# Two of four weight-block sums made in DRAM by a copy and an adding transfer, raw weights in tiles of 512 columns

## The chip, the cores and the metric

The kernel runs on one core of one Trainium2 chip. The metric is device time in microseconds (us) of one execution. Three runs of the kernel before gave 2002.77, 2003.87 and 2006.32 us; the median, 2003.87, is what the change is measured against.

## What is computed

One inference step of a two-layer encoder on 512 prompt and 32 sample positions (544 columns in the kernel), width 1024, all in fp32. Each layer is a half-step FFN, a mixer (pooling, short convolution, differential attention) with its projections, and a second half-step FFN, each followed by a LayerNorm of the scaled residual. The part that the change touches is the FFN's first product, `x @ w_in`:

```python
def swiglu(x, w_in, w_out):
    gate, up = jnp.split(x @ w_in, 2, axis=-1)
    return (jax.nn.silu(gate) * up) @ w_out

# encoder_layer, for each of DEPTH=2 layers (D_MODEL=1024, D_FF=2816)
x = layer_norm(ALPHA * x + 0.5 * swiglu(x, w_ffn_in[0], w_ffn_out[0]), ln_g[0], ln_b[0])
proj = x @ w_in
...
x = layer_norm(ALPHA * x + mix, ln_g[1], ln_b[1])
x = layer_norm(ALPHA * x + 0.5 * swiglu(x, w_ffn_in[1], w_ffn_out[1]), ln_g[2], ln_b[2])
```

## The kernel before

Features lie on the 128 partitions, positions on the free axis, cut in two halves of 272 columns. To keep fp32 accuracy every operand is split in a rounded high part and the remainder (`whi`, `wlo` for weights, `xh`, `xl` for activations), and each product takes three matmuls of 128 x 272: hi by hi, lo by hi, hi by lo. ScalarE rounds (L172 for weights), VectorE subtracts (L173).

Weights stream through one class, `Weights`, as a list of units in the order of use. A unit of kind "t" is a plain weight tile. A unit of kind "s" is one of the FFN's 22 column blocks from the fourth on (NPLAIN = 3): its weights are four blocks of 128 x 512 (b11, b12, b22, b21), and the function `seven` (L332, matmuls at L341) makes the 2 x 2 block product with seven products in place of eight, 84 matmuls. That needs four sums of weight blocks: r1 = b11 + b12, r2 = r1 + b22, r3 = b12 + b22 and r2 + b21, made by VectorE with `add` (L198, tiles `sum`), and sums of the activations (class `Blocks`, L316 to L319), made by VectorE when an FFN begins. There are 19 such units in each of four FFNs, 76 in all; they come in groups of six or seven, between which eight tiles of the FFN's second product (w2) stand.

Raw weights land in tiles `raw` of 128 x 1024, three of them (RAW_BUFS), by transfers that SP issues: L190 for plain tiles, L205 for the two of a sum unit. A raw tile is free again when its last `wlo` is made. The ten pairs of `whi` and `wlo` (W_BUFS) come free as TensorE uses them. So SP mostly waits for raw tiles.

Between FFNs stands a LayerNorm (class `LN`). Its last steps for the two halves go through all engines: VectorE centres and scales (z, L431), ScalarE applies gain and bias and rounds (L433, L438), POOL makes `xl` (L439), and TensorE begins the next weights' products on each of eight feature tiles as it comes (function `start`; three units at once). POOL has little else: rstd (L412), the LayerNorm's sums (L380, L381, L388) and small work in the mixer. A plain FFN block's activation is L591 (ScalarE) and L592 (VectorE), a sum unit's L552 to L567; the first of these, L552, copies a product to the tile `up`, and the third product, which adds to the same accumulator, waits for it. The split of an FFN's hidden tiles is L287 (hh) and L288 (hl).

The order of the instructions on each engine is set by the framework's scheduler from the written order and from priorities, and is fixed when the kernel is built. Each engine and each issuing queue works in order. At the start `first` (L215) loads three units and the activations in pieces; then SP loads parameters, and two small inputs of the bias table (L619, L620). The bias table itself is written to DRAM and spread there by one transfer (scr<-rows, L629).

Of the kernel before, what the change touches and what calls it, by code (L numbers as in the profile page):

```python
# [10 lines left out]
F32 = mybir.dt.float32  # L11
# [5 lines left out]
P = 128  # L17
# [18 lines left out]
FB = 5  # L36
W_BUFS = 10
RAW_BUFS = 3
# [10 lines left out]
G = 512  # L49
# [24 lines left out]
def encoder_kernel(  # L74
# [82 lines left out]
    class Weights:  # L157
# [4 lines left out]
        def __init__(self, units):  # L162
            self.units, self.used, self.loaded, self.ready = units, 0, 0, []

        def fetch(self):
            return wp.tile([P, 2 * G], F32, tag="raw", name="raw", bufs=RAW_BUFS)

# [14 lines left out]
        def load(self):  # L182
            kind, src, n = self.units[self.loaded]
            self.loaded += 1
            if kind == "t":
                raw = self.fetch()
                c = 0
                for part in src if isinstance(src, tuple) else (src,):
                    w = part.shape[-1]
                    nc.sync.dma_start(out=raw[:, c:c + w], in_=part)  # L190
                    c += w
                self.ready.append(Tile([self.group(raw[:, g:min(g + G, n)]) for g in range(0, n, G)]))
            else:
                self.ready.append(self.sums(src))

        def add(self, a, b):
            r = big["pool"].tile([P, G], F32, tag="sum", name="sum", bufs=4)
# [3 lines left out]
        def sums(self, src):  # L201

            raws = [self.fetch() for _ in range(2)]
            for i, raw in enumerate(raws):
                nc.sync.dma_start(out=raw, in_=src[:, 2 * i * G:2 * (i + 1) * G])  # L205
            b11, b12, b22, b21 = (raw[:, c:c + G] for raw in raws for c in (0, G))
            g11, g21 = self.group(b11), self.group(b21)
            r1 = self.add(b11, b12)
            r2 = self.add(r1, b22)
            g2, g1 = self.group(r2), self.group(r1)  # L210
            g3 = self.group(self.add(b12, b22))
            g22 = self.group(b22)
            return g11, g21, g2, g1, g3, g22, self.group(self.add(r2, b21))

        def first(self, x):  # L215

            units = self.units[:NSTART]
            raws = [self.fetch() for _ in units]
            tiles = [[self.new_group() for _ in range(2)] for _ in units]
            n = 2  # L220
            for i in range(NK // n):
                ks, cs = slice(n * i, n * i + n), slice(n * i * P, n * (i + 1) * P)
                nc.scalar.dma_start(out=ya[:, ks, HS[0]], in_=xT[:, ks, HS[0]])
                for raw, (_, src, _) in zip(raws, units):
                    o = slice(cs.start % G, cs.start % G + n * P)
                    nc.sync.dma_start(out=raw[:, cs], in_=src[cs.start // G][:, o])
            for i in range(NK // n):
# [926 lines left out]
```

## Time and profile before

| | |
|---|---|
| median of three runs | 2003.87 us (2002.77 to 2006.32) |
| profiled execution | 2006.03 us, its span 2004.2 us |
| TensorE, VectorE, ScalarE, POOL busy | 98%, 72%, 50%, 11% of the span |
| DMA | 189.12 MB moved, 94 GB/s in the mean |

The span runs from the first to the last instruction; 1.8 us of the execution's time lie outside it. Matmuls are pipelined, so one that lasts 0.29 us starts 0.125 us after the one before it, and the rate of starts tells more than busy time. A line of the profile is a line of the kernel before; PEld is TensorE's weight load, DVE is VectorE, ACT is ScalarE. In the order of the changed kernel, lines from 39 on have moved by some lines (L198 is now L223, L173 is L182, L439 is L459).

### The profile page before, as it was taken

The page shows a single profiled execution, that of the slowest core. Times are in us where ns is not written, and L with a number is a line of the kernel's source. Part 1 is how long each engine was busy: PE and PEld are TensorE (multiplying, and loading weights), DVE is VectorE, ACT ScalarE, POOL GpSimd, SP SyncE. Part 2 cuts the span into 40 slices and gives each one's busy share as a digit, 9 for nine tenths or more (in the row PEclk, how much of TensorE's full clock was granted, in tenths as well). Part 3 has the DMA queues.
Part 4 walks back from the last instruction along what each step waited for, and adds up shares of the span by engine and source line. Part 5 has one row for each costly group of instructions (what it writes and reads, how often), then busy time and mean ns, then how long its engine had stood idle before and what let it go on. Part 6 is the DMA issues. An engine that isn't in the chain of part 4 may idle for free.

```text
span 2004.2 us, 38173 instructions
## 1 busy us (share of the span) xinstructions
PE 1973.7 (98%) x15446; PEld 1937.3 (97%) x15446; DVE 1449.9 (72%) x2806; ACT 993.6 (50%) x2000; POOL 225.6 (11%) x214
## 2 busy tenths in 40 slices
PE   9999999999999999999999999999999999999997
PEld 9999999999899999999999999999899999999997
DVE  7958677677658967768798496775865698576676
ACT  6625445465436544535466254454754366355453
POOL 0000000510134000000420000015001330000003
PEclk9999999999899999999999999999999999999999
DMA  6332323142121242323223223232421213323231
GB/s 208 113 102 95 99 83 116 64 144 92 59 81 63 87 123 67 116 85 102 89 73 108 85 93 109 85 106 72 140 98 54 85 50 99 106 85 109 89 98 46
DMA packets 65834, 189.12 MB, mean 94 GB/s; under 512 B 9428, under 2 KB 15188, under 8 KB 65656
## 3 DMA queue, kind: packets, MB, share of 16 engines
q1 hardware_dynamic: 55584, 172.07, 27.4%
q10 hardware_dynamic: 10072, 14.60, 2.3%
q8 instruction: 121, 1.98, 0.4%
q14 instruction: 57, 0.47, 0.1%
HBM read 179.88 MB, written 8.34 MB: 94 GB/s over the span
## 4 chain that ended last, share of the span: by engine, by line
PE 90%; DVE 6%; issue 1%; ACT 1%; DMA 1%; POOL 1%; POOLq 0%; ACTq 0%; DVEq 0%
PE b L341 39%; PE b L255 30%; PE b L259 15%; DVE wlo L173 1%; PE b L778 1%; PE b L777 1%; DVE sum L198 1%; PE b L793 1%; PE b L419 1%; DVE z L431 1%; ACT ya L433 1%; PE b L865 1%; PE b L758 0%; DMA raw<-in_w 0%; PE b L405 0%
## 5 line engine op out<-in xcount | busy, mean ns | idle before, releaser
L172 ACT ACTIVATE whi<-raw 128x512 fp32r<-128x512 f32 (+2 forms) x586 | 357.3, 614 | 495.6 <-PE b L259 299.1
L173 DVE TENSOR_TENSOR wlo<-raw,whi 128x512 fp32r<-128x512 f32 (+2 forms) x586 | 408.8, 700 | 149.0 <-ACT whi L172 144.2
L255 PE MATMUL b<-hh,wlo 128*128 128x272 f32 x1408 | 405.7, 288 | 0.0
L255 PE MATMUL b<-hh,whi 128*128 128x272 f32 x1408 | 405.1, 288 | 0.0
L259 PE MATMUL b<-hl,whi 128*128 128x272 f32 x1408 | 404.7, 287 | 0.0
L255 PE MATMUL b<-xh,whi 128*128 128x272 f32 x1024 | 296.3, 297 | 10.0 <-ACT xh L438 9.1
L172 ACT ACTIVATE whi<-sum 128x512 fp32r<-128x512 f32 x304 | 190.7, 631 | 201.4 <-PE b L259 99.5
L255 PE MATMUL b<-xh,wlo 128*128 128x272 f32 x1024 | 290.1, 290 | 0.1
L173 DVE TENSOR_TENSOR wlo<-sum,whi 128x512 fp32r<-128x512 f32 x304 | 207.8, 689 | 87.4 <-ACT whi L172 80.4
L259 PE MATMUL b<-xl,whi 128*128 128x272 f32 x1024 | 265.7, 290 | 0.0
L255 PEld LDWEIGHTS b<-hh,whi 128*128 128x128 f32 x1408 | 265.0, 188 | 0.0
L255 PEld LDWEIGHTS b<-hh,wlo 128*128 128x128 f32 x1408 | 264.9, 188 | 0.0
L259 PEld LDWEIGHTS b<-hl,whi 128*128 128x128 f32 x1408 | 264.9, 188 | 0.0
L341 PE MATMUL b<-xh,wlo 128*128 128x272 f32 x912 | 262.6, 288 | 0.0
L341 PE MATMUL b<-xh,whi 128*128 128x272 f32 x912 | 262.2, 288 | 0.0
L341 PE MATMUL b<-xl,whi 128*128 128x272 f32 x912 | 261.8, 287 | 0.0
L255 PEld LDWEIGHTS b<-xh,whi 128*128 128x128 f32 x1024 | 195.1, 191 | 14.0 <-ACT xh L438 11.7
L255 PEld LDWEIGHTS b<-xh,wlo 128*128 128x128 f32 x1024 | 195.5, 191 | 0.6 <-DVE wlo L173 0.3
L259 PEld LDWEIGHTS b<-xl,whi 128*128 128x128 f32 x1024 | 182.3, 190 | 0.7 <-issue 0.5
L341 PE MATMUL b<-s56h,whi 128*128 128x272 f32 x608 | 175.4, 289 | 3.3 <-ACT up L552 3.3
L388 POOL TENSOR_TENSOR ya<-ya,shift 128x544 f32<-128x544 f32 x14 | 25.3, 1830 | 1355.4 <-DVE wlo L173 1313.9
L341 PE MATMUL b<-s73h,wlo 128*128 128x272 f32 x608 | 175.3, 288 | 0.0
(208 smaller groups left out, 4248.1 us busy)
## 6 DMA issues: line engine op xcount, KB each, us to landing
raw<-in_w SPq DMA_DIRECT2D x184, 512.0 KB, 3.8
raw<-in_w SPq DMA_DIRECT2D x64, 448.0 KB, 3.3
raw<-in_wi SPq DMA_DIRECT2D x40, 512.0 KB, 3.2
raw<-in_w SPq DMA_DIRECT2D x42, 256.0 KB, 3.3
raw<-in_wo SPq DMA_DIRECT2D x16, 512.0 KB, 3.2
U<-scr ACTq DMA_DIRECT2D x8, 320.0 KB, 3.5
out_nkT<-k ACTq DMA_DIRECT2D x8, 272.0 KB, 2.1
out_nvT<-vT ACTq DMA_DIRECT2D x8, 272.0 KB, 2.2
```

The source lines that it names most:

```text
L172: S.activation(out=hi, in_=raw, func=AF.Copy)
L173: V.tensor_tensor(out=lo, in0=raw, in1=hi.bitcast(F32), op=ALU.subtract)
L198: V.tensor_tensor(out=r, in0=a, in1=b, op=ALU.add)
L255: PE.matmul(acc[:, :HALF], v, x[k][0][:, HS[h]], start=first and i == 0, stop=False)
L259: PE.matmul(acc[:, :HALF], w.at(k)[0], x[k][1][:, HS[h]], start=False, stop=last)
L341: PE.matmul(acc[:, :HALF], v[:, cs], x, start=opens and j == 0 and m == 0, stop=j == len(xs) - 1 and m == 2, skip_group_check=True)
L388: POOL.tensor_tensor(out=c, in0=c, in1=self.s, op=ALU.subtract)
L419: PE.matmul(b[:, c * CH:(c + 1) * CH], self.rstd[h][:, c:c + 1].to_broadcast([CH, P]), ident[:CH, :CH], start=True, stop=True)
L431: V.tensor_tensor(out=z, in0=c, in1=self.rstd[h], op=ALU.mult)
L433: S.activation(out=c, in_=z, func=AF.Identity, bias=b, scale=g)
L777: PE.matmul(g[:, :w], qc[c][parts[c], qs], kh[parts[c], :w], start=True, stop=False)
L778: PE.matmul(g[:, :w], qc[c][:, qs], kc[c][:, :w], start=False, stop=True)
```

## The change

For the sum units from the third on (SUMS_FROM = 2), r1 and r3 are made in DRAM: SP copies b11 and b12 side by side into a DRAM tile `r13` of 128 x 1024 (L215), and POOL issues a transfer that adds b12 and b22 to it (L219). Both are written some units ahead (six and three), with a ring of eight DRAM tiles. The unit then loads five tiles of 128 x 512: b11, b21, b22 and the two halves of `r13`, and VectorE makes two sums, r2 and r2 + b21. All raw weights now land in tiles of 512 columns, seven of them, each by a transfer of its own. The mixer's buffers `f` go from five to four (FB), the `sum` buffers from four to three, and the bias table's two small loads go from SP's queue to ACT's.

```diff
@@ -33,9 +33,13 @@
 NB = 2
 NSTART = 3
 AHEAD = 300
-FB = 5
+SUMS_AHEAD = (6, 3)
+SUMS_FROM = 2
+FB = 4
 W_BUFS = 10
-RAW_BUFS = 3
+RAW_BUFS = 7
 FEED = (12, 5, 8)
 POOL_STATE = 15
 POOL_WINDOWS = (2, 4, 8, 16)
@@ -161,9 +165,14 @@
         def __init__(self, units):
             self.units, self.used, self.loaded, self.ready = units, 0, 0, []
-        def fetch(self):
-            return wp.tile([P, 2 * G], F32, tag="raw", name="raw", bufs=RAW_BUFS)
+            self.r13, self.ring = {}, []
+            self.todo = [[i for i, u in enumerate(units) if u[0] == "s"][SUMS_FROM:] for _ in range(2)]
+        def fetch(self, src):
+            raw = wp.tile([P, G], F32, tag="raw", name="raw", bufs=RAW_BUFS)[:, :src.shape[-1]]
+            nc.sync.dma_start(out=raw, in_=src)
+            return raw
         def new_group(self):
             return tuple(wp.tile([P, G], F32R, tag=n, name=n, bufs=W_BUFS) for n in ("whi", "wlo"))
@@ -182,56 +191,67 @@
         def load(self):
             kind, src, n = self.units[self.loaded]
             self.loaded += 1
+            self.sums_ahead()
             if kind == "t":
-                raw = self.fetch()
-                c = 0
-                for part in src if isinstance(src, tuple) else (src,):
-                    w = part.shape[-1]
-                    nc.sync.dma_start(out=raw[:, c:c + w], in_=part)
-                    c += w
-                self.ready.append(Tile([self.group(raw[:, g:min(g + G, n)]) for g in range(0, n, G)]))
+                parts = src if isinstance(src, tuple) else [src[:, g:min(g + G, n)] for g in range(0, n, G)]
+                self.ready.append(Tile([self.group(self.fetch(part)) for part in parts]))
             else:
-                self.ready.append(self.sums(src))
+                self.ready.append(self.seven(src, n, self.r13.pop(self.loaded - 1, None)))
+        def sums_ahead(self):
+            for ahead, todo, step in zip(SUMS_AHEAD, self.todo, (self.copy, self.accumulate)):
+                if todo and todo[0] < self.loaded + ahead:
+                    step(todo.pop(0))
+        def copy(self, i):
+            _, src, n = self.units[i]
+            if len(self.ring) < SUMS_AHEAD[0] + 2:
+                t = dram.tile([P, 2 * G], F32, name=f"r13_{len(self.ring)}")
+            else:
+                t = self.ring.pop(0)
+            self.ring.append(t)
+            self.r13[i] = t[:, :2 * n]
+            nc.sync.dma_start(out=self.r13[i], in_=src[:, :2 * n])
+        def accumulate(self, i):
+            _, src, n = self.units[i]
+            POOL.dma_start(out=self.r13[i], in_=src[:, n:3 * n], accum_op=ALU.add)
         def add(self, a, b):
-            r = big["pool"].tile([P, G], F32, tag="sum", name="sum", bufs=4)
+            r = big["pool"].tile([P, G], F32, tag="sum", name="sum", bufs=3)[:, :a.shape[-1]]
             V.tensor_tensor(out=r, in0=a, in1=b, op=ALU.add)
             return r
-        def sums(self, src):
-            raws = [self.fetch() for _ in range(2)]
-            for i, raw in enumerate(raws):
-                nc.sync.dma_start(out=raw, in_=src[:, 2 * i * G:2 * (i + 1) * G])
-            b11, b12, b22, b21 = (raw[:, c:c + G] for raw in raws for c in (0, G))
+        def seven(self, src, n, r13):
+            blocks = [src[:, :n], src[:, 3 * n:], src[:, 2 * n:3 * n]]
+            blocks += [src[:, n:2 * n]] if r13 is None else [r13[:, :n], r13[:, n:]]
+            b11, b21, b22, *b = (self.fetch(v) for v in blocks)
             g11, g21 = self.group(b11), self.group(b21)
-            r1 = self.add(b11, b12)
+            r1, r3 = b if b[1:] else (self.add(b11, b[0]), self.add(b[0], b22))
             r2 = self.add(r1, b22)
-            g2, g1 = self.group(r2), self.group(r1)
-            g3 = self.group(self.add(b12, b22))
-            g22 = self.group(b22)
+            g2, g1, g3, g22 = (self.group(v) for v in (r2, r1, r3, b22))
             return g11, g21, g2, g1, g3, g22, self.group(self.add(r2, b21))
...
@@ -616,8 +636,8 @@
     def build_bias(bp):
         rb = bp.tile([32, HEADS], F32, name="rb")
         oh = bp.tile([32, BL], F32, name="oh")
-        nc.sync.dma_start(out=rb, in_=relb)
-        nc.sync.dma_start(out=oh, in_=c_one)
+        nc.scalar.dma_start(out=rb, in_=relb)
+        nc.scalar.dma_start(out=oh, in_=c_one)
         vec = bp.tile([HEADS, BL], F32, name="vec")
         for q in range(2):
             acc, qs = bank(), slice(q * (BL // 2), (q + 1) * (BL // 2))
@@ -1023,7 +1043,7 @@
                     if i < NPLAIN:
                         units += [("t", (src[:, a * G:(a + 1) * G], src[:, b * G:(b + 1) * G]), 2 * G) for a, b in ((0, 3), (1, 2))]
                     else:
-                        units.append(("s", src, 4 * G))
+                        units.append(("s", src, G))
                 else:
                     c0, n = sum(FSPLIT[:i]) * P, FSPLIT[i] * P
                     units += [("t", w2[l, f, m, :, c0:c0 + n], n) for m in range(NK)]
```

The first place is VectorE where the second FFN of layer 0 begins: the last split of the weights before it (`wlo`), LayerNorm's `z`, the sums of the first sum unit, and the block sums of the activations (`s_...`). Before:

```order
L173 TENSOR_TENSOR wlo<-raw,whi 128x512
L411 TENSOR_SCALAR var<-var 68x4
L198 TENSOR_TENSOR sum<-raw 128x512
L431 TENSOR_TENSOR z<-ya,b 128x272 x8
L198 TENSOR_TENSOR sum<-sum,raw 128x512
L198 TENSOR_TENSOR sum<-raw 128x512
L198 TENSOR_TENSOR sum<-sum,raw 128x512
L316 TENSOR_TENSOR s_8052<-ya 128x272
L318 TENSOR_TENSOR s_8053<-ya 128x272
```

After:

```order
L182 TENSOR_TENSOR wlo<-raw,whi 128x512
L431 TENSOR_SCALAR var<-var 68x4
L451 TENSOR_TENSOR z<-ya,b 128x272 x8
L223 TENSOR_TENSOR sum<-raw 128x512
L223 TENSOR_TENSOR sum<-sum,raw 128x512
L336 TENSOR_TENSOR s_8261<-ya 128x272
L338 TENSOR_TENSOR s_8262<-ya 128x272
```

The adds r1 and r3 are gone: r2 (`sum<-raw`) and r2 + b21 stand behind the eight `z`, and the rest follows as before. The same pair is gone from the second unit, some 35 instructions later.

The second place is POOL in the LayerNorm ahead of that FFN. `xl` is the activations' remainder, eight tiles for each half. Before:

```order
L381 TENSOR_TENSOR acc_7261<-acc_7261,sq 128x544
L412 TENSOR_TENSOR rstd<-var,mhalf 68x4
L439 TENSOR_TENSOR xl<-ya,xh 128x272 x8
L412 TENSOR_TENSOR rstd<-var,mhalf 68x4
L439 TENSOR_TENSOR xl<-ya,xh 128x272 x8
L388 TENSOR_TENSOR ya<-ya,shift 128x544 x2
```

After, with `r_1_364` and the like as DRAM tiles of the ring:

```order
L432 TENSOR_TENSOR rstd<-var,mhalf 68x4
L459 TENSOR_TENSOR xl<-ya,xh 128x272 x8
L432 TENSOR_TENSOR rstd<-var,mhalf 68x4
L459 TENSOR_TENSOR xl<-ya,xh 128x272 x4
L219 DMA r_1_364<-in_w 128x1024
L459 TENSOR_TENSOR xl<-ya,xh 128x272 x4
L219 DMA r_2_437<-in_w 128x1024
L219 DMA r_3_567<-in_w 128x1024
```

One adding transfer now stands between the fourth and the fifth `xl` of the second half; the others of the FFN follow behind the eighth. The same stands ahead of the next two FFNs.

The third place is SP, from the mixer's weights (`in_wi`, `in_wo`) to the third sum unit of that FFN, after the change:

```order
L174 DMA raw<-in_wi 128x512 x40
L174 DMA raw<-in_wo 128x512 x16
L174 DMA raw<-in_w 128x512 x15
L174 DMA raw<-r_1_364 128x512 x2
L215 DMA r_1_364<-in_w 128x1024
L174 DMA raw<-in_w 128x512 x3
L174 DMA raw<-r_2_437 128x512 x2
L174 DMA raw<-in_w 128x512 x3
```

The copy into a ring tile stands right behind the loads from it for the unit that used it last, so the sums are begun eight units ahead.

## Rows read from the trace of the kernel before

**Rows 1.** The page: span, and busy time of each engine.

```profile
span 2004.2 us, 38173 instructions
...
PE 1973.7 (98%) x15446; PEld 1937.3 (97%) x15446; DVE 1449.9 (72%) x2806; ACT 993.6 (50%) x2000; POOL 225.6 (11%) x214
```

**Rows 2.** Windows: us; PE, PEld, DVE, ACT, POOL busy; granted clock; DMA share; GB/s.

```profile
160.00:230.00 70.00, 70.00 (x562) 70.00 (x561) 58.87 (x105) 42.62 (x80) 0.00 (x0) 1.00 0.34 102
634.00:665.00 31.00, 29.74 (x238) 29.52 (x237) 30.93 (x54) 21.89 (x44) 6.87 (x7) 1.00 0.21 66
```

**Rows 3.** Chain of waits, 655 to 666 us: start, us, what.

```profile
659.67 0.61 DVE sum L198
...
661.51 0.58 DVE sum L198
...
663.18 0.66 ACT hh L287
...
664.36 0.29 ACT up L552
...
664.70 1.39 PE b L341 x9
```

**Rows 4.** Timeline of TensorE (PE, then weight loads PEld), 663 to 666 us.

```profile
663.15 0.29 PE L341 MATMUL b<-xl,whi 128*128 128x272 f32 x1
...
664.70 0.19 PEld L341 LDWEIGHTS b<-s56h,whi 128*128 128x128 f32 x1 [1.48 <-ACT up L552]
```

**Rows 5.** Waits of TensorE's weight loads: us in total, times, longest.

```profile
PEld b L341 <- ACT up L552: 3.9, 3, 1.5
```

**Rows 6.** All instructions on tiles sum and raw: duration ns min/median/max.

```profile
L198 DVE TENSOR_TENSOR sum<-raw x152: 673/689/1267, 32.2 to 1918.3; 128x512 f32<-128x512 f32 x152
...
L205 SPq DMA_DIRECT2D raw<-in_w x152: 327/328/332, 21.4 to 1912.0; - x152
```

**Rows 7.** Timeline of VectorE, 626 to 642 us.

```profile
625.96 1.26 DVE L173 TENSOR_TENSOR wlo<-raw,whi 128x512 fp32r<-128x512 f32 x1
...
627.61 0.80 DVE L173 TENSOR_TENSOR wlo<-raw,whi 128x512 fp32r<-128x512 f32 x1
...
628.40 0.68 DVE L198 TENSOR_TENSOR sum<-raw 128x512 f32<-128x512 f32 x1
631.15 2.87 DVE L431 TENSOR_TENSOR z<-ya,b 128x272 f32<-128x272 f32 x8 [2.08 <-PE b L419]
...
635.13 1.26 DVE L198 TENSOR_TENSOR sum<-raw 128x512 f32<-128x512 f32 x1
```

**Rows 8.** DMA issues: KB each, median us to landing; window with the bias table's copy.

```profile
raw<-in_w SPq DMA_DIRECT2D x184, 512.0 KB, 3.8
...
raw<-in_w SPq DMA_DIRECT2D x42, 256.0 KB, 3.3
...
scr<-rows ACTq DMA_DIRECT2D x1, 1536.0 KB, 8.7
...
36.00:41.00 5.00, 5.00 (x43) 5.00 (x42) 5.00 (x11) 4.53 (x9) 0.00 (x0) 1.00 0.88 266
```

**Rows 9.** Timelines of POOL (xl) and TensorE, 632 to 643 us.

```profile
633.14 7.88 POOL L439 TENSOR_TENSOR xl<-ya,xh 128x272 fp32r<-128x272 f32 x8 [3.19 <-ACT xh L438]
...
635.80 2.40 POOL L439 TENSOR_TENSOR xl<-ya,xh 128x272 fp32r<-128x272 f32 x2
...
641.51 0.91 PE L259 MATMUL b<-xl,whi 128*128 128x272 f32 x6
```

**Rows 10.** Instructions on rstd (POOL) and on scr (issue by ACT), ns min/median/max.

```profile
L412 POOL TENSOR_TENSOR rstd<-var,mhalf x12: 1002/1014/1388, 375.8 to 1993.9; 68x4 f32<-68x4 f32 x12
...
L684 ACTq DMA_DIRECT2D U<-scr x8: 332/338/1434, 402.7 to 1457.9; - x8
```

**Rows 11.** Windows behind two equal waits of TensorE (columns as rows 2).

```profile
382.68:386.60 3.92, 3.92 (x22) 3.92 (x23) 3.37 (x7) 3.92 (x10) 3.42 (x4) 0.70 0.37 138
999.35:1003.00 3.65, 3.65 (x32) 3.62 (x33) 3.38 (x7) 3.65 (x10) 3.16 (x4) 1.00 0.46 150
```

More of the change, by code (lines that the diff above doesn't have):

```diff
@@ L217, in first @@
             units = self.units[:NSTART]
-            raws = [self.fetch() for _ in units]
+            raws = [[wp.tile([P, G], F32, tag="raw", name="raw", bufs=RAW_BUFS) for _ in range(2)] for _ in units]
             tiles = [[self.new_group() for _ in range(2)] for _ in units]
             n = 2
-            for i in range(NK // n):
-                ks, cs = slice(n * i, n * i + n), slice(n * i * P, n * (i + 1) * P)
+            cuts = [(n * i * P // G, slice(n * i * P % G, n * i * P % G + n * P)) for i in range(NK // n)]
+            for i, (g, cs) in enumerate(cuts):
+                ks = slice(n * i, n * i + n)
                 nc.scalar.dma_start(out=ya[:, ks, HS[0]], in_=xT[:, ks, HS[0]])
                 for raw, (_, src, _) in zip(raws, units):
-                    o = slice(cs.start % G, cs.start % G + n * P)
-                    nc.sync.dma_start(out=raw[:, cs], in_=src[cs.start // G][:, o])
-            for i in range(NK // n):
-                cs = slice(n * i * P, n * (i + 1) * P)
-                o = slice(cs.start % G, cs.start % G + n * P)
+                    nc.sync.dma_start(out=raw[g][:, cs], in_=src[g][:, cs])
+            for i, (g, cs) in enumerate(cuts):
                 for k in range(n * i, n * i + n):
@@ L232, in first @@
                 for raw, groups in zip(raws, tiles):
-                    hi, lo = groups[cs.start // G]
-                    self.part(raw[:, cs], hi[:, o], lo[:, o])
+                    hi, lo = groups[g]
+                    self.part(raw[g][:, cs], hi[:, cs], lo[:, cs])
             self.loaded, self.ready = len(units), [Tile(g) for g in tiles]
```

## Prediction

> **What bounds the kernel now.** I read the page's head first: TensorE is busy 98% of a span of 2004.2 us, VectorE 72% [rows 1]. A busy TensorE may still be waiting, so next come the windows, for the rate of its matmuls. In the 70 us from 160, a stretch of sum units (one column block of the first FFN product made with seven products), 562 matmuls run: one per 0.125 us, with no gap, while VectorE is busy 58.9 of 70 us and the DMA engines 0.34 of the time [rows 2]. There the kernel is bound by TensorE, and nothing that VectorE is spared can show. A unit is 7 x 4 x 3 = 84 matmuls, 10.5 us. The stretch 634 to 665 is different: 238 matmuls in 31 us, with VectorE busy 30.93 of 31.00 [rows 2]. This is the start of the second FFN of layer 0: LayerNorm is still being applied, the block sums of the activations (L316 to L319) are made, and the weights of the first sum units are prepared, all on VectorE. The chain of waits from 655 on shows what that does to TensorE: VectorE adds, an activation pair, ScalarE's split, its copy `up`, then matmuls [rows 3]. TensorE starts a matmul at 663.15 and the next at 664.70, released by `up` [rows 3, 4]. The waits list has three such waits, 3.9 us in all, the longest 1.5 [rows 5]; the two others end at the same place of the next two FFNs. Those 3.9 us are what a lighter VectorE can give back.
>
> **What the change takes away.** 74 of the 76 sum units lose two of their four adds, r1 and r3: 148 adds at 0.689 us [rows 6], 102 us of VectorE. In the stretches at TensorE's full rate that is worth nothing, since TensorE is the bound there. At the three places it counts. Of the first unit's four adds the one at 628.40 ran while VectorE waited for LayerNorm anyway (the next instruction, z, starts at 631.15), so its loss is free; the one at 635.13 took 1.26 us in the middle of the backlog [rows 7]. Of the second unit's four adds in the chain, two go, 0.61 and 0.58 us [rows 3]. In all about 2.4 us of backlog against a wait of 1.48 at most, so each wait should vanish; with the second unit's pair alone (1.2 us) the most that would be left is 0.3. The matmul starts give the loss: 664.70 - 663.15 less one spacing of 0.125 is 1.42, where the weight-load row reads 1.48 idle [rows 3, 4]; scaled to 3.9, **-3.7 us**. Bounds: -4.0 and, if only the second pair counts, -3.2.
>
> **What it adds, on SP.** Each sum unit now loads five tiles of 256 KB where it loaded two of 512 KB, and every other weight tile comes in two pieces: 832 SP transfers against 382, each 0.328 us of SP [rows 6], 148 us more on a queue that only waits for buffers otherwise. A copy stands behind the two loads of the ring buffer that it overwrites, so SP stands still until those land (3.3 us for 256 KB [rows 8]), with three raw loads of the unit after it queued behind. Seven raw buffers at five per 10.5 us hold 14.7 us of work; the cover is that slack. I take 0. If it is gone, a unit waits a few tenths, which is rival three's country.
>
> **What it adds, on POOL.** The accumulating transfers are issued from POOL, each after a wait for its copy. By the order all but three of them stand between LayerNorms, where POOL is idle. Three stand inside LayerNorm's second half, between the fourth and the fifth `xl`. Eight `xl` run from 633.14 for 7.88 us; the fourth and fifth end at 638.20, so POOL reaches the accumulate at about 637.0 and the eighth ends at 641.02 [rows 9]. TensorE reads the last two tiles from 641.51, the last one three matmuls (0.375 us) later, at 641.9 [rows 9]: 0.9 us to spare. Is the copy there by 637.0? Its ring buffer's second load needs the raw buffer freed by the wlo that ends at 628.41 [rows 7], lands 3.3 later at 631.7, and the copy then starts. Nothing in the trace is a copy of this size between DRAM tensors; the nearest is the bias table's, three times as large, 8.7 us [rows 8]. So 2.9 (a third) to 8.7; I take 3.8, the landing of a 512 KB load [rows 8], and have 635.5: before 637.0, so no wait. The issue itself is not in the trace either: between 0.33 us (a transfer issued by ACT) and 1.4 us (POOL's own smallest arithmetic, rstd, at its longest; median 1.0) [rows 10]. I take 1.0, the nearest on the same engine: 0.1 beyond the slack, three times, **+0.3 us**; bounds 0 and +1.5.
>
> **The rest.** The two bias loads move to ACT's queue, ahead of four splits: 2 x 0.34 us of ACT [rows 10], at a time when TensorE has three units' worth of weights in hand: 0, at most +0.7. FB 4, three sum buffers: the same order of instructions on POOL in the mixer, 0. DRAM traffic per unit grows from 1.05 MB to 1.31 of loads, 0.52 of copy and 0.52 (if an accumulate costs as a copy) to 1.57 (two reads and a write): 2.4 to 3.4 MB in 10.5 us. At 0.34 for 102 GB/s, and 0.88 for 266 while the bias table's copy runs [rows 2, 8], the engines move some 300 GB/s: 3.15 MB in 10.5 us. So the share goes to 0.75 to 1.08. The ring's eight buffers are filled far ahead, and between groups of six or seven sum units stand eight tiles of the second product; a load may land after 11 instead of 3.3 us before the 14.7 us of buffers run out (2 to 3 us of it is the split's). I take 0.
>
> **Sum.** 2006.03 - 3.7 + 0.3 = 2002.6, against the profiled execution's own time. That one lies 2.16 above the median of the three runs, 2003.87; on the median's scale the forecast is **2000.5 us**. Its own range, from the bounds above and one drop of the clock more or less, is 1998.5 to 2004. Such a drop: after a wait of the same 2.4 us the granted clock's mean was 0.70 in one place (part of it at the lower of the two levels, 1.2 GHz), with 22 matmuls in 3.92 us, and 1.00 in another, with 32 in 3.65 [rows 11]; it costs about 1.4 us where it falls.
>
> **Rivals.**
> *One: the waits stay.* VectorE's r2 now needs the ring buffer's tile, and everything at L316 to L319 stands behind it. Its load needs the raw tile freed by the wlo that ends at 627.2 and lands by 630.5; VectorE asks for it at 634.0, behind the eight z [rows 7]: 3.4 us to spare, which a load slowed by copies and accumulates could use up. Or an accumulate's issue is held while VectorE works, or holds it, as the adds and `xl` hold each other: an add takes 0.68 alone and 1.26 beside `xl` [rows 7]. One such hold per issue (1.26) costs 3 x 1.3 and eats the gain. Time: 2003.9, as before. For it: VectorE is never idle there. The Trainium skill, "SBUF — State Buffer", section "Who interferes with whom", warns that descriptors of a POOL transfer cannot be written while VectorE runs a two-port copy, and excepts tensor_tensor with two SBUF inputs, which it lets contend with POOL's reads alone. The trace agrees for reads (0.68 against 1.26); by that rule this half of the rival would fall and the forecast's 2000.5 stand. 0.22.
>
> *Two, slower: POOL stands in LayerNorm.* If the copy lands more than 5.2 us after its issue, POOL waits for it with four `xl` behind, and TensorE behind those, one for one. At the far bound of 8.7: 631.7 + 8.7 + 1.0 = 641.4 for the fifth `xl` instead of 637.0, 4.4 late, 3.5 beyond the slack, three times: +10.5, less 3.7: 2010.7. For it: TensorE has no other work in that place. Against it: DMA is 0.21 busy there [rows 2]. 0.18.
>
> *Three: the DMA engines.* At the upper bound of 1.08, 0.26 MB per unit are left over, 0.9 us; with nothing hidden, 74 x 0.9 = 64 us: about 2065. It decides where raw loads take over 11 us to land. The Trainium skill's page "DMA: Bandwidth & Descriptors", section "Issuing engines are not separate DMA queues", says that transfers of all issuers interleave on the same 16 engines, which speaks against this change: by it POOL's queue brings no bandwidth of its own, and the 64 us are the bound. The trace agrees as far as it goes, for SP's and ACT's transfers together (0.88 busy). Against it: the upper bound counts every passage of an accumulate at the price of a load, and the ring's lead of eight units has to be used up first. 0.07.
>
> *Four: not what it says.* The order shows 156 adds left of 304 and the copies eight units ahead, more than the six written. 0.01.
>
> **Chances.** Forecast 0.52, the rivals 0.22, 0.18, 0.07, 0.01. A measurement of this kernel tells 0.2%, 4 us, from no change: below 1999.86 is faster, above 2007.88 slower. A sum of 3.4 us lies next to the bound, so about half of the forecast is below 1999.86: faster 0.27. Same: the other half, the first rival, the fourth and the small cases of the second, 0.49. Slower: most of the second and the third, 0.24. The range leaves out the third rival and a tail at the low end: 1997 to 2011.
>
> **What would show it.** Right: 156 adds at the seven-product weights, no wait of L341's weight loads on `up` at the three places, 0.34 of DMA share grown to 0.75 or more with matmuls still at 0.125 us, `xl` at the three places with one gap of 1 us. Wrong: a POOL wait for a copy there, a wait of TensorE for whi or wlo inside sum units, raw loads that land after more than 11 us.

## Result and profile after: slower by 2.2%

The changed kernel took 2050.05 us in the median of four runs (2047.96 to 2050.34), the kernel before 2005.09 us on the same chip. The ratio is 1.0223, its 95% interval 1.0206 to 1.0241: slower by 45 us, where 2000.5 was forecast in a range from 1997 to 2011. The profiled execution took 2047.96 us.

The page of the changed kernel: span, busy time, DMA share in 40 slices, and two DMA queues (packets, MB, share of 16 engines); q1 is what SP issues, q0 the accumulates that POOL issues.

```profile
span 2046.2 us, 39606 instructions
...
PE 1986.7 (97%) x15446; PEld 1945.2 (95%) x15446; DVE 1365.4 (67%) x2658; ACT 995.4 (49%) x2000; POOL 281.6 (14%) x288
...
DMA  9966748333222665757428576662421228565331
...
q1 hardware_dynamic: 120576, 230.19, 37.3%
q0 software_dynamic: 10656, 38.80, 11.8%
```

Against [rows 1], VectorE is 84 us lighter, as the change meant, and the span is 42 us longer. So VectorE's time was not what was lost. Where it was lost the windows tell: the first 110 us of the kernel before, then the same 110 us and 70 us of sum units of the changed kernel (columns as in [rows 2]).

```profile
0.00:110.00 110.00, 107.66 (x827) 105.52 (x828) 92.17 (x190) 71.43 (x141) 0.20 (x4) 1.00 0.53 163
```

```profile
0.00:110.00 110.00, 95.44 (x674) 92.30 (x675) 74.92 (x158) 59.41 (x119) 10.15 (x16) 0.92 0.94 259
...
187.00:257.00 70.00, 65.86 (x507) 65.64 (x507) 48.21 (x88) 38.61 (x73) 4.06 (x5) 0.95 0.74 187
```

In the first 110 us 674 matmuls start instead of 827; 153 at 0.125 us are 19 us. In the 70 us from 187 it is 507 instead of the 562 that start in 70 us of sum units of the kernel before [rows 2], 6.9 us, and this was the kind of stretch in which TensorE had no gap before. The DMA engines are busy 0.94 and 0.74 of the time, where it was 0.53 and 0.34.

What TensorE waits for is in the waits of the changed kernel (L223 is the add, L587 a step of a sum unit's activation that reads its fifth product, L361 the matmuls of `seven`, L182 the split into `wlo`, L215 the copy, L174 the raw loads; SPq is SP's queue).

```profile
DVE sum L223 <- DMA raw<-r: 131.4, 57, 6.4
PEld b L361 <- DVE sg L587: 26.5, 21, 4.4
...
PEld b L361 <- DVE wlo L182: 5.6, 2, 5.2
...
SPq L215 <- DMA raw<-r: 102.7, 41, 5.4
```

VectorE waits 131 us for loads of the ring's tiles, and TensorE for `sg` of VectorE, a wait that [rows 5] did not have beside it; once, at 73.69 us, it waits 5.2 us for the `wlo` of a sum unit. How the one makes the other is in VectorE's timeline, 220 to 231 us, and in the chain of waits of the same place.

```profile
220.21 0.69 DVE L182 TENSOR_TENSOR wlo<-raw,whi 128x512 fp32r<-128x512 f32 x1
227.32 0.69 DVE L223 TENSOR_TENSOR sum<-raw 128x512 f32<-128x512 f32 x1 [6.41 <-DMA raw<-r]
227.93 0.43 DVE L584 TENSOR_TENSOR up<-b,up 128x272 f32<-128x272 f32 x1
...
230.68 0.43 DVE L587 TENSOR_TENSOR sg<-sg,b 128x272 f32<-128x272 f32 x1
```

```profile
220.97 6.25 DMA raw<-r
...
230.76 0.36 DVE sg L587
...
231.17 1.95 PE b L361 x7
```

VectorE works in order. It stands 6.4 us at r2 of a later unit, because r1's load, issued at 220.97, takes 6.25 us. Behind that add in its queue stand `up` and `sg` of the unit that TensorE is working on now, so TensorE stops: its last matmul of this stretch starts at 226.74, the next at 231.17. From 229.7 to 236.5 the granted clock is 0.50, the lower of its two levels (1.2 GHz):

```profile
229.70:236.50 6.80, 5.33 (x23) 5.33 (x24) 5.17 (x10) 1.85 (x3) 0.81 (x1) 0.50 0.85 245
```

So a part of the loss is paid in clock. Leaving out the last 20 us, 159 matmuls start in stretches at this level, in the kernel before 93. An estimate of the most that this can be: 66 more at a spacing longer by 0.125 us are 8 of the 42 us.

The landing times have grown (KB each, median us to landing; [rows 8] had 3.3 for a load of 256 KB):

```profile
raw<-in_w SPq DMA_DIRECT2D x400, 256.0 KB, 4.1
r<-in_w SPq DMA_DIRECT2D x74, 512.0 KB, 5.5
r<-in_w POOLq DMA_DIRECT2D x74, 512.0 KB, 6.7
raw<-r SPq DMA_DIRECT2D x148, 256.0 KB, 3.8
```

The start of the kernel is the worst place: the order puts the first eight copies and accumulates there, beside the first weights and the bias table. The chain of waits, 26 to 110 us:

```profile
21.21 13.00 DMA raw<-in_w
...
41.68 23.78 DMA scr<-rows
65.53 0.33 SPq L174
...
66.03 4.90 DMA raw<-r
...
72.87 8.52 DMA raw<-in_w
```

A raw load takes 13.0 us, and the bias table's copy 23.8 where it took 8.7 [rows 8]. Eight raw loads of `in_w` take more than 11 us in this trace, all of them issued in the first 56 us; in the kernel before the longest took 7.2.

### The profile page after: what moved, and what is told of

It is laid out like the page before. It is cut to its first block, busy times and chain, and to the rows that moved or that the text cites. A ratio compares the mean times of both kernels' runs of the same rounds, so it can differ in the third digit from the quotient of the medians.

```text
span 2046.2 us, 39606 instructions
## 1 busy us (share of the span) xinstructions
PE 1986.7 (97%) x15446; PEld 1945.2 (95%) x15446; DVE 1365.4 (67%) x2658; ACT 995.4 (49%) x2000; POOL 281.6 (14%) x288
## 3 DMA queue, kind: packets, MB, share of 16 engines
q0 software_dynamic: 10656, 38.80, 11.8%
## 4 chain that ended last, share of the span: by engine, by line
PE 79%; DVE 8%; DMA 8%; issue 2%; ACT 1%; POOL 0%; SPq 0%; DVEq 0%; POOLq 0%; ACTq 0%
PE b L361 31%; PE b L275 28%; PE b L279 14%; DMA raw<-r 5%; DVE wlo L182 3%; DMA raw<-in_w 2%; DMA scr<-rows 1%; PE b L798 1%; PE b L797 1%; PE b L813 1%; DVE sum L223 1%; DVE s L338 1%; ACT ya L453 1%; PE b L439 1%; PE b L778 0%
## 5 line engine op out<-in xcount | busy, mean ns | idle before, releaser
L181 ACT ACTIVATE whi<-raw 128x512 fp32r<-128x512 f32 (+2 forms) x734 | 450.1, 617 | 590.9 <-PE b L279 331.9
L182 DVE TENSOR_TENSOR wlo<-raw,whi 128x512 fp32r<-128x512 f32 (+2 forms) x734 | 509.6, 697 | 205.1 <-ACT whi L181 196.0
L275 PE MATMUL b<-xh,whi 128*128 128x272 f32 x1024 | 297.4, 298 | 14.0 <-ACT xh L458 9.1
L361 PE MATMUL b<-xh,whi 128*128 128x272 f32 x912 | 267.6, 294 | 22.0 <-DVE sg L587 21.9
L361 PE MATMUL b<-xh,wlo 128*128 128x272 f32 x912 | 265.8, 292 | 5.2 <-DVE wlo L182 5.2
L361 PE MATMUL b<-xl,whi 128*128 128x272 f32 x912 | 264.3, 290 | 0.0
L275 PEld LDWEIGHTS b<-xh,whi 128*128 128x128 f32 x1024 | 196.0, 191 | 18.5 <-ACT xh L458 12.0
L219 POOL DMA_DIRECT2D r<-in_w x74 | 60.5, 817 | 1064.5 <-DMA r<-in_w 1038.1
L361 PEld LDWEIGHTS b<-xh,whi 128*128 128x128 f32 x912 | 174.3, 191 | 26.5 <-DVE sg L587 26.5
L275 PEld LDWEIGHTS b<-xh,wlo 128*128 128x128 f32 x1024 | 196.4, 192 | 0.6 <-DVE wlo L182 0.3
L361 PEld LDWEIGHTS b<-xh,wlo 128*128 128x128 f32 x912 | 174.9, 192 | 5.6 <-DVE wlo L182 5.6
L361 PE MATMUL b<-s56h,whi 128*128 128x272 f32 x608 | 175.4, 289 | 2.0 <-ACT up L572 2.0
L361 PE MATMUL b<-s73h,wlo 128*128 128x272 f32 x608 | 176.0, 290 | 0.0
```

The lines of the kernel that those rows point to most:

```text
L181: S.activation(out=hi, in_=raw, func=AF.Copy)
L182: V.tensor_tensor(out=lo, in0=raw, in1=hi.bitcast(F32), op=ALU.subtract)
L219: POOL.dma_start(out=self.r13[i], in_=src[:, n:3 * n], accum_op=ALU.add)
L275: PE.matmul(acc[:, :HALF], v, x[k][0][:, HS[h]], start=first and i == 0, stop=False)
L361: PE.matmul(acc[:, :HALF], v[:, cs], x, start=opens and j == 0 and m == 0, stop=j == len(xs) - 1 and m == 2, skip_group_check=True)
```

## Experiments

The theory from these views: **copies and accumulates fill the DMA engines in bursts, loads then land late, and VectorE, in order, passes that on to TensorE.** Rivals: the smaller raw tiles, SP standing in front of its copies, a fixed price for each pair of copy and accumulate wherever it stands, or bad luck of the start alone. The table reads each profile against the kernel before: how much later the same matmul starts (single profiles; a negative number is earlier). Its columns are the matmul that starts at 101.6 us before, one near the first FFN's end (369), one near the mixer's end (631), and the last of all (1996).

| run | ratio and interval | 101.6 | 369 | 631 | end |
|---|---|---|---|---|---|
| the change | 1.0223 [1.0206, 1.0241] | 19.2 | 27.3 | 25.4 | 42.3 |
| e1 tiles only | 0.9994 [0.9985, 1.0003] | 0.8 | 0.8 | -2.6 | -2.5 |
| e2 no DRAM sums | 0.9975 [0.9964, 0.9986] | 0.3 | 0.3 | -3.0 | -7.0 |
| e3 no accumulate | 0.9992 [0.9982, 1.0001] | 1.8 | 1.8 | 0.0 | -1.4 |
| e4 copy on POOL | 1.0241 [1.0210, 1.0272] | 36.8 | 39.6 | 37.8 | 43.5 |
| e5 late start | 1.0172 [1.0145, 1.0199] | 0.6 | 0.6 | 17.2 | 34.1 |
| e6 late start, POOL | 1.0130 [1.0107, 1.0152] | -0.4 | -0.4 | 8.4 | 22.9 |
| e7 two copies | 1.0110 [1.0083, 1.0136] | 7.9 | 11.6 | 8.3 | 18.7 |
| e8 six sums | 1.0032 [1.0023, 1.0042] | -0.1 | -0.1 | 10.0 | 5.5 |
| e9 six, spread | 0.9975 [0.9966, 0.9984] | -0.4 | -0.4 | -3.8 | -4.9 |
| e10 start only | 1.0052 [1.0033, 1.0070] | 11.4 | 11.4 | 9.5 | 12.7 |
| e11 ring of 16 | 1.0420 [1.0388, 1.0453] | 55.6 | 62.9 | 59.6 | 92.4 |
| e12 less ahead | 1.0124 [1.0107, 1.0141] | 9.4 | 12.2 | 10.2 | 19.6 |

Part of the columns comes from the one profile of the kernel before. Between 369 and 631 its granted clock stood at 0.50 for 13.6 us (384.2 to 387.6 and 520.8 to 531.0), that of e1 and e2 for 6.8. So e1, which has no DRAM sum, gains 3.4 us there, and what e5, e6 and e8 lose in the mixer is larger than the columns show, by up to as much.

All diffs are against the changed kernel.

### Which part costs: e1, e2, e3, e7

e1 keeps the tiles of 512 columns and makes all four sums on VectorE:

```diff
-SUMS_FROM = 2
+SUMS_FROM = 99
```

> The changed kernel with SUMS_FROM = 99: raw tiles of 512 columns and seven buffers stay, all four adds are VectorE's again, no copy and no accumulating transfer. Three theories of the 45 us. Traffic (copies and accumulates fill the DMA engines, at the start above all, and make every load land later): 2000 to 2006, as the kernel before. SP's queue (a copy stands in it until the loads from its ring tile land, 102.7 us in all): also 2000 to 2006. Ring (seven tiles of 512 at five per unit give a unit's last loads too little lead, whatever else runs): 2008 to 2020, with VectorE still waiting for raw tiles in its adds, since four loads per unit take half of the lead back.

No difference from before: the tiles, SP's more issues (684 here, 382 before, 832 in the change) and the two loads moved to ACT cost nothing, as the prediction took them, and the ring theory falls.

e2 has the two adds per unit and the five loads, but no copy and no accumulate: b12 and b22 themselves are loaded in the place of r1 and r3.

```diff
-            self.sums_ahead()
...
-                self.ready.append(self.seven(src, n, self.r13.pop(self.loaded - 1, None)))
+                i = self.loaded - 1
+                late = i in self.todo[0]
+                self.ready.append(self.seven(src, n, src[:, n:3 * n] if late else None))
```

> The changed kernel without any copy or accumulating transfer: from the third sum unit on, the halves of the ring tile are loaded from the input instead (b12 and b22 stand in for r1 and r3, so the products are not the reference's). Five loads and two adds per unit as in the changed kernel. Traffic and SP's queue: 1998 to 2003, the three waits at the FFNs' beginnings gone and the adds never waiting for a load. Ring: 2010 to 2030, with VectorE's add waiting for the fourth and fifth load in many units.

2000.28 us, 4.8 faster than before and 3.9 faster than e1: the lighter VectorE is worth what the prediction said, once nothing is paid for it. At the starts of the second, third and fourth FFN the gain can be read by itself, between the matmuls that in the kernel before start at 655, 1035 and 1650 us and those at 667, 1045 and 1660: they come 1.5, 1.1 and 1.5 us closer together, 4.1 in all. In e1, with all four sums on VectorE, it is 0.6, nearly all of it at the second start. The window of e2 in a stretch of sum units shows what five loads per unit ask of the DMA engines, 0.43 against 0.34 [rows 2]:

```profile
160.00:230.00 70.00, 70.00 (x562) 70.00 (x562) 54.23 (x97) 42.38 (x80) 0.00 (x0) 1.00 0.43 126
```

e3 leaves the accumulates out (r1 and r3 are then b11 and b12), e7 puts a second plain copy in their place (r1 and r3 are b12 and b22):

```diff
-            POOL.dma_start(out=self.r13[i], in_=src[:, n:3 * n], accum_op=ALU.add)
+            pass
```

> The changed kernel without the accumulating transfers (r1 and r3 are then b11 and b12): copies on SP stay, with their wait in the queue. Traffic: the accumulates hold 11.8% of the engines against some 8% of the copies, so half or more of the loss goes, 2020 to 2030, most of it at the start. SP's queue: 2040 to 2050, nearly unchanged in the sum units, since each copy still stands behind its loads. Ring: 2040 to 2050.

```diff
-            POOL.dma_start(out=self.r13[i], in_=src[:, n:3 * n], accum_op=ALU.add)
+            POOL.dma_start(out=self.r13[i], in_=src[:, n:3 * n])
```

> The changed kernel with the accumulating transfer replaced by a plain copy of the same source to the same place, from POOL, at the same point (r1 and r3 are then b12 and b22, so the products are not the reference's). If the accumulate's own price counts (328 ns per packet against 159): the loss falls to a third or less, 2008 to 2020. If it is enough that POOL has a transfer there and loads wait for it: 2040 to 2050.

The 74 copies alone cost 4.0 us (2004.30 against e2's 2000.28), and the accumulates some 46 more. With a plain copy in their place a little under half of that is left (2025.12). Neither was expected: e3 lies below all three of its theories, e7 between its two. The page of e7, the same queue q0 with the same packets and bytes, and the landing of its transfers:

```profile
q0 software_dynamic: 10656, 38.80, 6.3%
...
r<-in_w POOLq DMA_DIRECT2D x74, 512.0 KB, 5.0
```

An accumulate takes 11.8% of 2046.2 us over 74, 3.26 us of all sixteen engines; a plain copy of the same bytes 6.3% of 2022.7 over 74, 1.72 us. So 20.8 us of the loss come with a second transfer for each unit, on a third queue, and 24.9 with its being an accumulate. What differs between the two pages is that it holds the engines nearly twice as long as a copy, and lands in 6.7 us instead of 5.0; that the hold alone makes the 24.9 is argued, not shown.

### Whether the place matters: e4, e5, e6, e10

e4 issues the copies from POOL, so that SP never stands in front of one:

```diff
-            nc.sync.dma_start(out=self.r13[i], in_=src[:, :2 * n])
+            POOL.dma_start(out=self.r13[i], in_=src[:, :2 * n])
```

> The changed kernel with the copies issued by POOL ahead of the accumulates, nothing else. SP's queue: the 102.7 us that SP stood before copies are gone, the adds' 131 us of waiting for ring tiles fall to under 50, time 2020 to 2035. Traffic: the same bytes, 2043 to 2055. Ring: 2040 to 2055.

The total is the changed kernel's, as the traffic theory had it, but the loss has moved: 37 us at the start, where the copies now come earlier still (the first at 1.25 us instead of 11.85), and 7 behind it where the change lost 23. VectorE's waits for the ring's tiles fall only to 103.8 us. This doesn't separate SP's waits from the traffic, since POOL in order also keeps copy and accumulate from running together.

e5 lets the DRAM sums begin with the second FFN, and holds the ring's tiles back (a transfer of one column, from a tile of the first mixer) until the mixer; e6 is e5 with the copies on POOL.

```diff
-SUMS_FROM = 2
+SUMS_FROM = 19
+NRING = 8
...
+        def gate(self, t):
+            for r in self.ring:
+                POOL.dma_start(out=r[:, :1], in_=t[:, :1])
...
+            if l == 0 and h == 0:
+                W.gate(kt)
```

> The changed kernel without DRAM sums in the first FFN (SUMS_FROM = 19), and the ring's tiles are first written (one column) from the first mixer's key tile, so that no copy can be issued before it. Copies on SP, accumulates on POOL as in the changed kernel. Start theory (19 us are lost by the 760th matmul because the first eight copies and accumulates run while the first weights land): nothing lost before the mixer; behind it what the changed kernel lost from there on, 15 us: 2018 to 2022. Rival (the burst costs the same wherever it stands): 19 us are lost in the mixer instead, 2035 to 2045.

> As the late start, and the copies are issued by POOL. In the run with the copies on POOL the kernel lost only 4 us from the first mixer on. If SP's queue, standing before copies, makes the waits inside sum units: 2007 to 2012. If the accumulates' load on the engines makes them alone: as the late start with copies on SP, 2018 to 2022.

Nothing is lost at the start any more, and 17 us in the mixer, where the eight pairs now come at once: as the rival had it, the burst costs about as much in another place. With POOL's copies it costs half, 8.8 us. But no copy stands in SP's queue in e6, and from the mixer's end on it still loses 14.5 us where e5 loses 16.9; its 2030.27 lies above both theories. The windows of e5, 415 to 460 us:

```profile
415.00:460.00 45.00, 35.18 (x209) 30.86 (x207) 21.38 (x51) 17.58 (x46) 6.78 (x10) 0.85 1.03 271
```

e10 makes the DRAM sums for the first eight units alone:

```diff
-            self.todo = [[i for i, u in enumerate(units) if u[0] == "s"][SUMS_FROM:] for _ in range(2)]
+            self.todo = [[i for i, u in enumerate(units) if u[0] == "s"][SUMS_FROM:10] for _ in range(2)]
```

> The change as it stands, with the DRAM sums for the first eight of its 74 units alone: the eight pairs that the order puts in the first 100 us. All other sum units make four sums on VectorE from four loads. Burst theory: the loss of the first 100 us stays (19 us in the changed kernel), and nothing is lost or gained later, since the units behind have no copies about them: ratio 1.0095 (1.007 to 1.012), some 2024 us. Rival, a price per pair: 8 x 0.6 = 5 us, ratio 1.0025. Second rival, the loss at the start was time that the kernel has in hand there and would be made good later: ratio 1.000.

11.4 us are lost in the first 100 us, and nothing behind them, as the burst theory had it. Both rivals lie outside the interval. But the measured ratio lies below the theory's range as well, which the interval's upper end just reaches: the eight pairs by themselves cost 11 us, not 19. In the changed kernel the copies for the ninth unit and those behind it are issued from 71.6 us on, into the same 100 us, which may be the rest; that was not tried by itself.

### A version that keeps the gain: e8 and e9

Only the first two sum units of an FFN need a lighter VectorE. e8 makes the DRAM sums for these six alone, each with a tile of its own, held back until the mixer as in e5:

```diff
-SUMS_FROM = 2
+SUMS_AT = (19, 20, 38, 39, 57, 58)
+NRING = 6
...
+            s = [i for i, u in enumerate(units) if u[0] == "s"]
+            self.todo = [[s[j] for j in SUMS_AT] for _ in range(2)]
```

> DRAM sums only for the first two sum units of the second, third and fourth FFN, six in all, each with a ring tile of its own, copied and summed in the first mixer (its tiles first written from the key tile as in the late start); all other units make four adds, raw tiles of 512. If the gain of the run without DRAM sums (4 to 5 us) comes from these six units alone: 1999 to 2002. If it needs the lighter VectorE everywhere, or six accumulates in the mixer cost something there: 2003 to 2006.

By the matmuls named for e2 the three starts gained 1.5, 1.1 and 1.5 us. But the six pairs come as one burst, the mixer loses 10, and the time, 2011.65, lies above both theories. The chain of waits of e8, 415 to 450 us, shows the price of one load in it:

```profile
420.90 21.69 DMA raw<-in_wi
...
445.53 1.22 PE b L818 x4
```

e9 issues the same six pairs from POOL one at a time, three in each of the first two groups of second-product tiles of the first FFN, where the DMA engines were busy 0.24 and 0.25 of the time:

```diff
+        def sums_ahead(self, t):
+            i = self.todo.pop(0)
             _, src, n = self.units[i]
+            self.r13[i] = dram.tile([P, 2 * G], F32, name=f"r13_{i}")
+            POOL.dma_start(out=self.r13[i][:, :1], in_=t[:, :1])
+            POOL.dma_start(out=self.r13[i], in_=src[:, :2 * n])
             POOL.dma_start(out=self.r13[i], in_=src[:, n:3 * n], accum_op=ALU.add)
...
                 for h in range(2):
                     resid(m, acc[h], h, i == 0)
+                if l == 0 and f == 0 and m in (1, 3, 5):
+                    W.sums_ahead(y[m])
```

> The six sum units of e8 once more (the first two of the second, third and fourth FFN), each with a DRAM tile of its own, but now one at a time: in the first FFN, while the first and second groups of tiles of its second product run, POOL issues for each tile a transfer of one column that waits for a finished piece of the residual, then the copy, then the accumulate. Those two stretches lie at 110 to 160 and 232 to 280 us, where the kernel before keeps its DMA engines busy for 0.24 and 0.25 of the time. Burst theory (copies and accumulates cost where many of them and the unit's loads fill the engines together): nothing is lost there, raw loads land in about 3.2 us, the share in the two stretches rises to about 0.35, and the gains at the three FFN starts stand (e8: -1.5, -1.0, -2.0): 2000.6 on this scale, ratio 0.9977 (0.9965 to 0.999). Rival, each pair costs on its own wherever it stands (45 us over 74 pairs, 0.6 us a pair): +3.6 against -4.5: ratio 0.9995, no difference from before.

1999.93 us against 2004.59: 0.25% faster than the kernel before, with 1 outside the interval. Its windows of the two stretches, and its queue q0, which holds all copies and accumulates here:

```profile
110.00:160.00 50.00, 50.00 (x402) 50.00 (x402) 23.84 (x43) 11.56 (x19) 6.14 (x9) 1.00 0.56 136
232.00:280.00 48.00, 48.00 (x387) 48.00 (x386) 26.47 (x50) 13.75 (x24) 5.86 (x9) 1.00 0.63 149
...
q0 software_dynamic: 1920, 6.30, 1.5%
```

Not a matmul is lost: 402 and 387, as before, and a fixed price for each pair wherever it stands falls (by it the ratio was to be 0.9995). The share rose to 0.56 and 0.63, not to the 0.35 expected: 1.5% of 1999.5 us over six pairs are 5.0 us of all engines for each, the sum of the 3.26 and 1.72 measured above. The three starts gained 1.5, 1.1 and 1.5 us, and no weight load of the sum units waits for `up` any more, where [rows 5] had 3.9 us.

### How far ahead: e11 and e12

e11 has a ring of sixteen tiles, e12 writes copies and accumulates three and two units ahead, which makes the ring five tiles:

```diff
-            if len(self.ring) < SUMS_AHEAD[0] + 2:
+            if len(self.ring) < 16:
```

> The change with a ring of sixteen DRAM tiles in place of eight, so that a copy overwrites a tile whose loads were issued sixteen sum units ago: SP's wait of copies for the ring's loads (102.7 us in 41 waits in the changed kernel) should all but vanish, while the traffic stays the same. The order then puts some sixteen pairs, not eight, into the first 100 us. Theory that the loss after the start (23 us behind the 19 of the first 100 us) is SP standing in front of copies with raw loads behind it: it falls to under 8 us. Rival, traffic: copies and accumulates that run beside a unit's loads slow them whatever SP waits for: 15 to 25 us stay. By either the start costs more than 19 us, 25 to 35 us, since twice as many pairs stand there. Total: 2035 to 2045 us (ratio 1.016 to 1.020) by the first, 2045 to 2062 (1.021 to 1.029) by the second.

```diff
-SUMS_AHEAD = (6, 3)
+SUMS_AHEAD = (3, 2)
```

> The change with copies written three units ahead and accumulates two (six and three in the change), so with a ring of five tiles. By the order five pairs, not eight, stand at the start, and copies come closer behind the loads that free their tile. Burst theory: the loss of the first 100 us falls to about five eighths, 12 us. SP theory: a smaller ring makes SP stand longer in front of copies, so the loss behind the start grows from 23 us to 30 or more. Traffic rival: the loss behind the start stays at 20 to 25 us. Total: 2042 us or more (ratio from 1.0185) by the SP theory, 2034 to 2040 us (1.0145 to 1.0175) by the traffic rival.

e11 was a miss on both sides: worse than either theory, 56 us at the start and 37 behind. Its premise didn't hold either, since SP's wait did not vanish. In SP's waits of e11 it grew, from 102.7 to 131.6 us; the second line is the same wait in e3, which has the copies and no accumulate:

```profile
SPq L215 <- DMA raw<-r: 131.6, 39, 30.2
```

```profile
SPq L215 <- DMA raw<-r: 65.4, 46, 3.3
```

The order moves each copy forward until it stands right behind the loads that free its tile, whatever the ring's length. e12 goes the other way: the start loses 9.4 us (12 expected), what is behind it 10 (20 to 25 by the traffic rival, 30 or more by the SP theory), and SP stands 85.5 us. Both theories had expected more. A shorter lead is better in both parts. The SP theory had standing and loss grow with a smaller ring, and both shrank; but since they went together (85.5, 102.7 and 131.6 us against 10, 23 and 37 behind the start), these two runs don't decide against it. e3 and e6 do: SP stands 65.4 us in e3 and the kernel is as fast as before, and in e6 SP never stands before a copy and 14.5 of e5's 16.9 us behind the mixer stay. Whether standing adds to the loss once accumulates run beside it is open. Why the loss behind the start grows with the ring as well (10, 23, 37 us for 5, 8, 16 tiles) stays open: the longer ring lets more copies run ahead beside a group's own loads, but no run holds the number of pairs in flight apart from SP's place in the queue.

## Why the prediction was wrong

**The gain was right.** -3.7 us for three waits; e2, e8 and e9 give -4.1 each at the three starts, e1 -0.6 of it without any DRAM sum. In the changed kernel itself it is -0.5, -1.0 and -0.7 at the waits, and some 20 us later late loads have taken it back: +0.2, +0.8 and +0.9, counted from the same matmuls ahead of the starts. The wait for `up` is still there at two of the three (0.94 and 0.73 us).

**POOL was right.** The issue inside LayerNorm was put at 1.0 us against a slack of 0.9. POOL's timeline of the changed kernel, 655 to 667 us:

```profile
658.55 3.88 POOL L459 TENSOR_TENSOR xl<-ya,xh 128x272 fp32r<-128x272 f32 x4 [3.19 <-ACT xh L458]
662.49 0.91 POOL L219 DMA_DIRECT2D r<-in_w  x1
663.15 3.23 POOL L459 TENSOR_TENSOR xl<-ya,xh 128x272 fp32r<-128x272 f32 x4
```

The issue takes 0.91 us there (0.84 and 0.88 at the other two places, 0.80 to 1.00 over all 74), and no wait for the copy stands between the `xl`: rival two did not come. Nor is an issue held by VectorE's adds, though VectorE is busy 67% of the span. The Trainium skill, "SBUF — State Buffer", section "Who interferes with whom", says that tensor_tensor takes only the read side of the port pair that VectorE shares with POOL, and infers that this leaves the writing of descriptors free; the trace agrees (0.80 to 1.00 us).

**What failed is "I take 0" for the DMA engines.** That term measured 50 us: e2, which has all of the change but its copies and accumulates, takes 2000.28 us where the sum said 2000.5, and the changed kernel 2050.05. (The same words for SP were off by 4.0 us at most, which is what the copies on SP's queue cost in e3, traffic and standing together.) The share that it worked out, 0.75 to 1.08, was about right (0.74 in a stretch of sum units, with TensorE standing in part of it). Three things in the step were wrong.

*The price of an accumulate* was left between 0.52 and 1.57 MB and then put aside. It can be read now: 3.26 us of all engines, 1.9 times a copy of the same bytes. An estimate from these figures: with e2's share for five loads, the pair and the loads ask for 0.43 x 10.5 + 3.26 + 1.72 = 9.5 of a unit's 10.5 us. That leaves no room for anything that comes in a bunch.

*The point from which it decides* was put at loads that land after 11 us, by the stock of raw buffers that TensorE has. In the first 56 us eight raw loads did land later than that, which was the prediction's own sign of being wrong. Behind the start none did, and time was lost all the same: there the first to starve is VectorE, in order, which asks for r1 well before TensorE needs r2, with `up` and `sg` of the present unit behind. A landing of 6.25 us was enough, as the chain at 220.97 shows. The first rival had seen this wait ("a load slowed by copies and accumulates could use up"), but at the three FFN starts alone, and priced at the gain; it happens all along. What costs is its length, not the count: in e2 VectorE waits 58 times for these loads, 42.6 us in all and 1.8 at most, and TensorE doesn't notice; in the changed kernel it is 57 times, 131.4 us and 6.4 at most, and TensorE stands behind it 21 times. Whether VectorE would be out of trouble with r2's add placed behind `sg`, or with more raw buffers, was not tried.

*The ring's lead of eight units was counted as cover.* It is the burst itself: eight pairs as early as the order can place them, at the kernel's most crowded time. By the first 100 us, 19 of the 42 us between the two profiles are lost; the eight pairs by themselves cost 11 (e10). The prediction used the bias table's copy as a price for a transfer, and did not ask what runs beside that copy.

So the time lies between the forecast and rival three's 2065, and the limit is the third's, the DMA engines; it had a chance of 0.07. That 45 us lie so near its 64 is luck: its sum had the engines asked for more than they can do in every unit, and they were asked for 9.5 of 10.5 us; the loss came from bunches and from VectorE's order. SP's loads of 256 KB landed in 4.1 us in the median beside POOL's queue, and in 3.2 in e2 without it. The rule named there, from the Trainium skill's "DMA: Bandwidth & Descriptors", section "Issuing engines are not separate DMA queues", is that transfers run on the same 16 engines whichever engine started them; the trace agrees (4.1 against 3.2). That was weighed in the right direction, and then overruled by an argument on buffers that no row had borne out.

## What to carry to other kernels

Work that is moved to the DMA engines is paid there in engine time: take the packets' share of one such transfer (here 3.26 us for an accumulate, 1.72 for a copy of 512 KB) against what a unit of work has left, before counting buffers. Ask who reads the late load first, and what stands behind that reader in its queue, not how long the last consumer can live from its stock. And "far ahead" without a gate means "all at once at the earliest moment": six pairs in one burst cost 10 us, the same six one at a time in a quiet stretch cost nothing.

## What was not expected of the hardware

An accumulating transfer between DRAM tensors keeps the engines busy 1.9 times as long as a plain copy of the same bytes (11.8% against 6.3% of the span on one queue). And in a burst a load's landing grows sevenfold: 21.7 us for 256 KB that take 2.9 in the median of the same kernel.
